# An encoder layer in float32: the low parts of half of the w_up blocks made in an earlier stage and kept in DRAM

## The chip, the cores and the metric

The kernel runs on one core of one Trainium2 chip. The metric is the time of one execution on the device, in microseconds (us), of a program that has all inputs in DRAM and writes both outputs to DRAM. A core has five engines with an instruction queue each: PE (matrix products), DVE (vector), ACT (scalar functions and casts), POOL (a second vector engine) and SP (which only issues transfers). Each engine takes its instructions in order; semaphores order the engines among each other. DMAs are issued by SP and ACT on hardware queues and by POOL on a software queue.

## The reference

One layer for 1536 tokens (512 of a prompt and 1024 of a sample), model width 1024, hidden width 4096, in float32. What the change touches is the last part:

```python
h = rms_norm(x, g_mix)
...
merged = jax.nn.sigmoid(ga) * (attn @ w_branch_a) + jax.nn.sigmoid(gb) * (sgu @ w_branch_b)
x = x + merged @ w_out
h2 = rms_norm(x, g_mlp)
x = x + jnp.square(jax.nn.relu(h2 @ w_up)) @ w_down
...
return rms_norm(x, g_final)
```

## The kernel before

**Products.** Every operand of a float32 product is split into a high part, hi (ACT casts it to float32r), and a rest, lo (DVE subtracts: lo = raw - hi). A product is then three matmuls: hi by hi, hi by lo and lo by hi. `weight` (L156) loads a weight tile of 128x512 (256 KB) with SP into a ring of three buffers (`raw`, N_RAW = 3), lets ACT cast it (L153) and DVE subtract (L154) into rings of five (`hi`, `lo`, N_SPLIT = 5). A raw buffer is free when ACT and DVE have both read it, hi and lo when PE has used them.

**Stages.** Projections, spatial gating and attention fill 0 to 1184 us; gates and the two branches, in three chunks of 512 tokens, 1184 to about 1614; w_out, the residual and the norm up to about 1770; the MLP the rest. In the gates stage a chunk has 14 gate products of 24 matmuls, 8 products of branch a of 12 and 8 of branch b of 24.

**MLP.** Both products use a scheme with seven products in place of eight for 2x2 blocks. The seven forms are p1, p2, q3 and q4 to q7; the sums of weight blocks for q4 to q7 (`up_sums`, `down_sums`) are made by DMA during attention. Group g (two, 768 tokens each) runs over c = 0 to 7; each c has two blocks of `up_products`, here called even (j = 0) and odd (j = 1), of seven weights each in the order p1, q6, q7, p2, q5, q4, q3 (UP_ORDER), 12 matmuls of 384 columns per weight, and then `down_products` with 14 weights. Names with a prime below: p1', q6' are weights of the odd block.

Between the products of an up block the results are combined and split: p1 is copied by ACT (L933); v = q6 - p1 (L936), z = v - q7 (L943); a11 is the squared Relu of p1 + p2 (ACT L915, L916), then cast (ACT) and subtracted (DVE) into act; a22 = z + q5 (DVE L946), a21 (L951), a12 (L956), and sums of them (L862 to L873) likewise. q3 accumulates on the PSUM bank of q5, so PE may start q3 only when DVE has read q5 for a22. In `down_products` POOL adds z to two tiles after q7 (L995, L996) and the kept p to one after q3 (L1006).

**Forms of the normed rows.** h2 (the normed rows, transposed) is stored to `h2_scr`; `diff_steps` reads it back and stores sums of blocks to `form_scr`. `form_steps` loads the seven forms of a group with POOL (`raw_form`, L1026, 28 loads) and splits them into `hf`. For group 0 that happens ahead of and within the first up block; for group 1 in the odd block and the down products of the last c of group 0. In group 1 POOL also loads finished rows of group 0 (`row`, L1061) and the gain (`g_final`, L240) and stores the normed rows.

**What sets the order.** Instructions stand in program order as written, moved by the scheduler of the tile framework; `side` steps are dealt out one after each product. The waits come from the buffers' rings.

Of the kernel before, what the change touches and what calls it, by code (L numbers as in the profile page):

```python
# [10 lines left out]
F32 = mybir.dt.float32  # L11
# [97 lines left out]
def encoder_kernel(ctx: ExitStack, tc: tile.TileContext, a):  # L109
# [25 lines left out]
    gate_scr = [dram.tile([P, NTOK], F32, name=f"gate_scr{m}") for m in range(EARLY)]  # L135
    form_scr = [dram.tile([len(DIFFS), 4, P, HT], F32, name=f"form_scr{g}") for g in range(2)]
    row_scr = dram.tile([GT, DM], F32, name="row_scr")
    h2_scr = dram.tile([KB, P, NTOK], F32, name="h2_scr")
    x1_scr = dram.tile([NTOK, DM], F32, name="x1_scr")
    up_sums = {k: dram.tile([DM // 2, DFF // 2], F32, name=f"up_{k}") for k in SUMS}  # L140
    down_sums = {k: dram.tile([DFF // 2, DM // 2], F32, name=f"down_{k}") for k in SUMS}
# [11 lines left out]
        nc.scalar.copy(hi, src)  # L153
        eng.tensor_sub(lo, src, hi.bitcast(F32))  # L154

    def weight(src, k, pair=None, eng=nc.vector):  # L156

        raw = wp.tile([P, 512], F32, tag="raw", name="raw", bufs=N_RAW).rearrange("p (k n) -> p k n", k=k)
        nc.sync.dma_start(out=raw, in_=src.rearrange("(k p) n -> p k n", p=P))
        if pair is None:  # L160
            pair = (wp.tile([P, 512], F32R, tag=s, name=s, bufs=N_SPLIT) for s in ("hi", "lo"))
        hi, lo = (t.rearrange("p (k n) -> p k n", k=k) for t in pair)
        split(hi, lo, raw, eng)
        return hi, lo

    def stationary(src, col, nk):
# [3 lines left out]
    def product(out, terms):  # L170

        for _ in product_steps(out, terms):
            pass
# [470 lines left out]
    def resident2(name):  # L644
        return res2.tile([P, 4, 512], F32R, tag="res2", name=name)

    with ExitStack() as ph:
        fp = ph.enter_context(tc.tile_pool(name="gates", bufs=20))
        rp = ph.enter_context(tc.tile_pool(name="rows", bufs=1))

        def half_tile(name):
            return fp.tile([P, 512], F32, tag="half", name=name)

        def merge_attention(t):

            r = rp.tile([P, NG, NPAIR, ROW], F32, tag="rows", name="rows")
            for g in range(NG):
                nc.sync.dma_start(out=r[:, g], in_=o_scr[g][t * P:(t + 1) * P])
            low = r[:, :, :, 128:130]
            den = r[:, :, :, 130:132]  # L660
            m = small.tile([P, NPAIR, 2], F32, tag="m", name="m")
            nc.vector.tensor_tensor(out=m, in0=low[:, 0], in1=low[:, 1], op=ALU.min)
            nc.vector.tensor_tensor(out=m, in0=m, in1=low[:, 2], op=ALU.min)
            e = small.tile([P, NG, NPAIR, 2], F32, tag="e", name="e")
            for g in range(NG):
                nc.vector.tensor_sub(e[:, g], m, low[:, g])
            nc.scalar.activation(e, e, AF.Exp)
            s = small.tile([P, NG, NPAIR, 2], F32, tag="s", name="s")
            for g in range(NG):
                nc.vector.tensor_mul(s[:, g], e[:, g], den[:, g])  # L670
            nc.vector.tensor_add(m, s[:, 0], s[:, 1])
            m2 = small.tile([P, NPAIR, 2], F32, tag="m2", name="m2")
            nc.vector.tensor_add(m2, m, s[:, 2])
            nc.vector.reciprocal(m2, m2)
            for g in range(NG):
                nc.vector.tensor_mul(e[:, g], e[:, g], m2)
            att, tmp = half_tile("att"), half_tile("att_g")
            for g in range(NG):
                dst = (tmp if g else att).rearrange("p (q h c) -> p q h c", q=NPAIR, h=2)
                nc.vector.tensor_mul(  # L680
                    dst, r[:, g, :, 0:128].rearrange("p q (h c) -> p q h c", h=2),
                    e[:, g, :, :, None].to_broadcast([P, NPAIR, 2, 64]))
                if g:
                    nc.vector.tensor_add(att, att, tmp)
            return att

        for n in range(NCH):
            sig = {}
            attT = tuple(resident2(f"att_{s}") for s in "hl")
            for i in range(2 * KB):  # L690
                s, m = divmod(i, KB)
                if i % 3 == 0 and i < 12:
                    att = merge_attention(4 * n + i // 3)
                sig[s, m] = half_tile("sig")
                if i < EARLY:
                    acc = sig[s, m]
                    nc.sync.dma_start(out=acc, in_=gate_scr[m][:, n * 512:(n + 1) * 512])
                else:
                    w = stationary(w_in, (C_GB, C_GA)[s] + m * P, KB)
                    acc = acc_tile()  # L700
                    product(acc, feature_terms(w, hT[n]))
                nc.scalar.activation(sig[s, m], acc, AF.Sigmoid)
                if i % 3 == 2 and i < 12:
                    to_features(att, [attT], 4 * n + i // 3)
            sgu = resident()
            for k in range(KB):
                raw = half_tile("sgu_raw")
                nc.sync.dma_start(out=raw, in_=sgu_scr[k][:, n * 512:(n + 1) * 512])
                hi, lo = sgu[k // 4]
                split(hi[:, k % 4, :], lo[:, k % 4, :], raw)  # L710
            for m in range(KB):
                w = stationary(a["w_branch_a"][0], m * P, 4)
                acc = acc_tile()
                product(acc, feature_terms(w, [attT]))
                nc.vector.tensor_mul(sig[1, m], acc, sig[1, m])
            for m in range(KB):
                w = stationary(a["w_branch_b"][0], m * P, KB)
                acc = acc_tile()
                product(acc, feature_terms(w, sgu))
                nc.vector.tensor_mul(sig[0, m], acc, sig[0, m])  # L720
                nc.vector.tensor_add(sig[0, m], sig[0, m], sig[1, m])
            hT[n] = resident()
            for m in range(KB):
                hi, lo = hT[n][m // 4]
                split(hi[:, m % 4, :], lo[:, m % 4, :], sig[0, m])
# [13 lines left out]
    def h_features(t, halves):  # L739

        for i, h in enumerate(halves):
            pt = tp_tile()
            for b in range(4):
                nc.tensor.transpose(pt[:, b * P:(b + 1) * P], h[:, b * P:(b + 1) * P], ident)
            hT2 = pp.tile([P, 512], F32, tag="half", name="h2T", bufs=2)
            nc.vector.tensor_mul(
                hT2.rearrange("p (k t) -> p k t", k=4), pt.rearrange("p (k t) -> p k t", k=4),
                g_mlp[:, 4 * i:4 * i + 4, None].to_broadcast([P, 4, P]))
            nc.sync.dma_start(
                out=h2_scr[4 * i:4 * i + 4, :, t * P:(t + 1) * P].rearrange("k p t -> p k t"),  # L750
                in_=hT2.rearrange("p (k t) -> p k t", k=4))

    def diff_steps(g, k, new, eng, wait):
# [2 lines left out]

        def load(key, r, s):
            x[key] = new()
            eng.dma_start(out=x[key], in_=h2_scr[4 * s + k, :, g * GT + r * HT:g * GT + (r + 1) * HT])

        def store(form, key):
            eng.dma_start(out=form_scr[g][DIFFS.index(form), k], in_=x[key])
# [26 lines left out]
    for k in range(4):  # L789

        room = [x1[(2 * k + i // 2) % 6][:, i % 2 * HT:(i % 2 + 1) * HT] for i in range(4)]
        sums += diff_steps(0, k, lambda room=room: room.pop(0), nc.gpsimd, 0)
    for ch in range(2):
        cols = slice(ch * 512, (ch + 1) * 512)
        w = {}
# [103 lines left out]
    def slab_view(s):  # L899
        return s.rearrange("p a b c -> p (a b c)").bitcast(F32)[:, :DM]  # L900

    def block_of(w, sums, form, rows, cols, r, c):

        if form in SUMS:
            return sums[form][r, c]
        i, j = {"p1": (0, 0), "p2": (1, 0), "q3": (1, 1)}[form]
        return w[i * rows + r.start:i * rows + r.stop, j * cols + c.start:j * cols + c.stop]

    def up_products(hf, j, forms, between):

        c = slice(j * P, (j + 1) * P)
        held = {}

        def squared(x, src):
# [1 line left out]
            nc.scalar.activation(x, x, AF.Square)  # L916

        for form in UP_ORDER:
            w = weight(block_of(a["w_up"][0], up_sums, form, DM // 2, DFF // 2, slice(0, DM // 2), c), 4)
            on = {"p2": "p1", "q3": "q5"}.get(form)  # L920
            acc = held[on] if on else bank()
            held[form] = acc
# [88 lines left out]
    def form_source(g, form, k):  # L1011
        if form in DIFFS:
            return form_scr[g][DIFFS.index(form), k]
        r, s = {"p1": (0, 0), "p2": (0, 1), "q4": (1, 1)}[form]
        return h2_scr[4 * s + k, :, g * GT + r * HT:g * GT + (r + 1) * HT]

    def form_steps(g, fs):

        items = [(form, k) for form in UP_ORDER for k in range(4)]
        raws = {}  # L1020

        def step(i):
            for j in range(i, min(i + N_FORM, len(items))):
                if j not in raws:
                    raws[j] = unit("raw_form")
                    nc.gpsimd.dma_start(out=raws[j], in_=form_source(g, *items[j]))  # L1026
            form, k = items[i]
            fs[k].put(form, raws[i])

        return [lambda i=i: step(i) for i in range(len(items))]  # L1030
# [131 lines left out]
```

## Time and profile before

| | us |
|---|---|
| median of three runs | 2805.28 (2803.55 to 2806.35) |
| profiled execution | 2803.75 |
| its span, first to last instruction | 2802.0 |
| PE busy | 2692.5 |
| DVE busy | 1747.7 |
| ACT busy | 1290.1 |
| POOL busy | 422.5 |

The mean granted PE clock over the span is 0.986 of full speed. A PE matmul of 384 columns in the MLP takes 0.17 us of its queue, an up block's weight (12 of them) 2.1 us. In the profile's rows, "x" counts instructions, the name ahead of "<-" is what is written, behind it what is read (buffer numbers left out), and square brackets give how long the engine stood idle before the row and what ended that.

### The profile page before, as it was taken

How to read it: one execution, taken by the hardware profiler on the slowest of the kernel's cores; microseconds unless marked ns; L12 is line 12 of the kernel's file. 1: busy time of each engine (PE TensorE's matmuls, PEld its weight loads, DVE VectorE, ACT ScalarE, POOL GpSimd, SP SyncE). 2: the span in 40 equal slices, each digit the busy share in tenths (PEclk: the TensorE clock that was granted, in tenths of full speed). 3: DMA queues.
4: the chain of work that ended last, by engine and by line, in shares of the span. 5: the costliest groups of instructions: out<-in, count | busy, mean ns of one | idle time of the engine just before them, and what ended most of it. 6: DMA issues, size and time to landing. Idle time of an engine off the chain costs nothing.

```text
span 2802.0 us, 38921 instructions
## 1 busy us (share of the span) xinstructions
PE 2692.5 (96%) x13400; PEld 2309.0 (82%) x13400; DVE 1747.7 (62%) x3722; ACT 1290.1 (46%) x2766; POOL 422.5 (15%) x507
## 2 busy tenths in 40 slices
PE   7999999999999999999999999899999989999997
PEld 5788888888888887888888887788989878888886
DVE  5542200166666666556555526788888868888888
ACT  5421111255556566553434321555556545555555
POOL 1000000011121212100000002222211322222222
PEclk9999999999999999999999999899999989999998
DMA  3112222247576768554443437654544555444443
GB/s 128 53 49 75 89 76 79 87 112 179 151 176 180 174 174 193 132 153 140 136 144 119 141 118 244 229 150 146 152 143 129 161 189 156 141 142 136 139 143 128
DMA packets 376439, 391.16 MB, mean 140 GB/s; under 512 B 23088, under 2 KB 290352, under 8 KB 372656
## 3 DMA queue, kind: packets, MB, share of 16 engines
q1 hardware_dynamic: 337008, 253.85, 30.3%
q0 software_dynamic: 28112, 86.83, 12.8%
q10 hardware_dynamic: 11120, 47.98, 5.0%
q8 instruction: 106, 1.74, 0.3%
q14 instruction: 93, 0.76, 0.1%
HBM read 333.22 MB, written 122.45 MB: 163 GB/s over the span
## 4 chain that ended last, share of the span: by engine, by line
PE 35%; DVE 8%; DMA 6%; issue 4%; ACT 4%; POOL 3%; DVEq 0%; SPq 0%; ACTq 0%; POOLq 0%
PE acc L979 7%; PE acc L178 7%; PE acc L180 7%; PE acc L179 7%; PE acc L928 6%; DVE lo L154 3%; DMA raw<-up_q 3%; ACT hi L153 1%; POOL x L996 1%; POOL x L995 1%; DVE act L154 1%; DMA raw<-in_w_down_dram 1%; ACT a L916 1%; ACT a L915 1%; ACT act L153 1%
## 5 line engine op out<-in xcount | busy, mean ns | idle before, releaser
L154 DVE TENSOR_TENSOR lo<-raw,hi 128x512 fp32r<-128x512 f32 x695 | 556.2, 805 | 420.8 <-ACT hi L153 413.8
L153 ACT CAST hi<-raw 128x512 fp32r<-128x512 f32 x696 | 430.6, 619 | 686.4 <-PE acc L179 238.3
L178 PE MATMUL acc<-res_h,hi 128*128 128x512 f32 x1344 | 556.2, 414 | 0.8 <-DVE stg L579 0.8
L180 PE MATMUL acc<-res_h,lo 128*128 128x512 f32 x1344 | 526.5, 392 | 0.0
L179 PE MATMUL acc<-res_l,hi 128*128 128x512 f32 x1344 | 525.3, 391 | 0.0
L928 PE MATMUL acc<-hf,hi 128*128 128x384 f32 x1792 | 471.6, 344 | 46.0 <-DVE a L946 24.8
L979 PE MATMUL acc<-hi,act 128*128 128x512 f32 x1344 | 423.9, 395 | 6.6 <-ACT hi L153 6.6
L928 PEld LDWEIGHTS acc<-hf,hi 128*128 128x128 f32 x1792 | 331.8, 193 | 59.2 <-ACT hi L153 30.8
L979 PEld LDWEIGHTS acc<-hi,act 128*128 128x128 f32 x1344 | 255.6, 191 | 61.4 <-ACT hi L153 8.9
L928 PE MATMUL acc<-hf,lo 128*128 128x384 f32 x896 | 306.1, 342 | 0.0
L180 PEld LDWEIGHTS acc<-res_h,lo 128*128 128x128 f32 x1344 | 252.4, 188 | 54.5
L179 PEld LDWEIGHTS acc<-res_l,hi 128*128 128x128 f32 x1344 | 254.3, 189 | 36.0
L178 PEld LDWEIGHTS acc<-res_h,hi 128*128 128x128 f32 x1344 | 254.0, 189 | 36.4 <-DVE stg L579 0.9
L979 PE MATMUL acc<-lo,act 128*128 128x512 f32 x672 | 266.1, 396 | 5.1 <-DVE lo L154 5.1
L551 ACT ACTIVATE pr<-pr,stg 128x128 f32<-128x128 f32 (+2 forms) x288 | 125.9, 438 | 175.8 <-DVE stg L548 139.5
L928 PEld LDWEIGHTS acc<-hf,lo 128*128 128x128 f32 x896 | 172.9, 193 | 0.9 <-DVE lo L154 0.8
L979 PEld LDWEIGHTS acc<-lo,act 128*128 128x128 f32 x672 | 128.3, 191 | 34.5 <-DVE lo L154 8.0
L521 DVE TENSOR_TENSOR q<-qT,q 64x256 fp32r<-64x256 f32 x288 | 120.7, 419 | 47.7 <-ACT q L518 43.9
L573 PEld LDWEIGHTS o<-v,pT 128*128 128x128 f32 x896 | 120.4, 191 | 24.9 <-DVE pT L563 14.7
L563 DVE COPY pT<-tp 128x512 f32<-128x512 f32 (+1 forms) x144 | 82.2, 571 | 93.9 <-PE tp L561 92.8
L995 POOL TENSOR_TENSOR x<-x,z 128x512 f32<-128x512 f32 x48 | 70.5, 1469 | 426.9 <-DVE z L994 426.8
L573 PE MATMUL o<-v,pT 128*128 128x64 f32 x896 | 117.3, 268 | 7.9 <-DVE pT L563 7.7
(186 smaller groups left out, 4119.9 us busy)
## 6 DMA issues: line engine op xcount, KB each, us to landing
raw<-in_w_in_dram SPq DMA_DIRECT2D x192, 256.0 KB, 3.0
raw<-up_q SPq DMA_DIRECT2D x128, 256.0 KB, 2.9
raw<-down_q SPq DMA_DIRECT2D x128, 256.0 KB, 2.7
raw<-in_w_up_dram SPq DMA_DIRECT2D x96, 256.0 KB, 2.9
raw<-in_w_down_dram SPq DMA_DIRECT2D x96, 256.0 KB, 2.9
up_q<-in_w_up_dram POOLq DMA_DIRECT2D x32, 512.0 KB, 9.3
down_q<-in_w_down_dram POOLq DMA_DIRECT2D x32, 512.0 KB, 10.9
raw<-in_w_branch_b_dram SPq DMA_DIRECT2D x48, 256.0 KB, 2.8
```

Source lines behind the costliest of these rows:

```text
L153: nc.scalar.copy(hi, src)
L154: eng.tensor_sub(lo, src, hi.bitcast(F32))
L178: nc.tensor.matmul(out, sh, mh, start=i == 0, stop=False)
L179: nc.tensor.matmul(out, sh, ml, start=False, stop=False)
L180: nc.tensor.matmul(out, sl, mh, start=False, stop=i == n - 1)
L521: nc.vector.tensor_sub(q2[rows, h, 1, :], src, q2[own, h, 0, :].bitcast(F32))
L551: last_of["act"] = nc.scalar.activation(pr[:, h, at:at + kn], pr[:, h, at:at + kn], AF.Exp, bias=low, scale=-1.0, accum_out=stg[:, j, 130 ...
L563: nc.vector.tensor_copy(self.pT[:, :n], pt[:, :n])
L573: nc.tensor.matmul(o[:, (2 * j + h) * 64:(2 * j + h + 1) * 64], self.pT[:, q * P:(q + 1) * P], found["v"][:, slot, h * 64:(h + 1) * 64], s ...
L928: nc.tensor.matmul(acc, st, mv, start=not on and k == 0 and n == 0, stop=k == 3 and n == 2, skip_group_check=bool(on))
L979: nc.tensor.matmul(acc, st, mv, start=not on and k == 0 and n == 0, stop=k == 1 and n == 2, skip_group_check=bool(on))
L995: nc.gpsimd.tensor_sub(x21, x21, z)
```

## The change

It has five parts.

1. In the gates stage `next_rest` runs after each of the gate products and the branch-b products: it takes the block of w_up loaded at the call before, casts it (ACT), subtracts (DVE), stores the rest to DRAM (`up_rest`) with POOL, and issues the load of the next block with POOL. 56 blocks, the seven forms of the eight odd j, are made that way, at 66 call places.
2. In the MLP the odd blocks' weights get lo by a POOL DMA from `up_rest` into the same ring, in place of DVE's subtraction: 7 per c, 112 in all. The raw load on SP and ACT's cast stay.
3. `h2_scr` becomes one tensor for each group.
4. The loads of each of the four lists of `diff_steps` for group 0 stand four places earlier in `sums`.
5. The 28 form loads of group 1 are issued by SP, those of group 0 still by POOL. `block_of` moves up unchanged and gets a helper, `up_block`.

```diff
-    h2_scr = dram.tile([KB, P, NTOK], F32, name="h2_scr")
+    h2_scr = [dram.tile([KB, P, GT], F32, name=f"h2_scr{g}") for g in range(2)]
+    up_rest = dram.tile([len(FORMS), DFF // 2 // P // 2, P, 512], F32R, name="up_rest")
...
-    def weight(src, k, pair=None, eng=nc.vector):
+    def weight(src, k, pair=None, eng=nc.vector, rest=None):
...
-        split(hi, lo, raw, eng)
+        if rest is None:
+            split(hi, lo, raw, eng)
+        else:
+            nc.scalar.copy(hi, raw)
+            nc.gpsimd.dma_start(out=lo, in_=rest.rearrange("p (k n) -> p k n", k=k))
...
+        rests = [(form, j) for j in range(1, DFF // 2 // P, 2) for form in FORMS]
+        loaded = []
+
+        def next_rest():
+
+            if loaded:
+                form, j, raw = loaded.pop()
+                t = fp.tile([P, 512], F32R, tag="rest", name="rest", bufs=2)
+                nc.scalar.copy(t, raw)
+                nc.vector.tensor_sub(t, raw, t.bitcast(F32))
+                nc.gpsimd.dma_start(out=up_rest[FORMS.index(form), j // 2], in_=t)
+            if rests:
+                form, j = rests.pop(0)
+                raw = fp.tile([P, 512], F32, tag="whole", name="whole", bufs=1)
+                nc.gpsimd.dma_start(
+                    out=raw.rearrange("p (k n) -> p k n", k=4), in_=up_block(form, j).rearrange("(k p) n -> p k n", p=P))
+                loaded.append((form, j, raw))
...
                     product(acc, feature_terms(w, hT[n]))
+                    next_rest()
...
                 product(acc, feature_terms(w, sgu))
+                next_rest()
...
-        sums += diff_steps(0, k, lambda room=room: room.pop(0), nc.gpsimd, 0)
+        steps = diff_steps(0, k, lambda room=room: room.pop(0), nc.gpsimd, 0)
+
+        sums.insert(max(0, len(sums) - 4), steps[0])
+        sums += steps[1:]
...
-            w = weight(block_of(a["w_up"][0], up_sums, form, DM // 2, DFF // 2, slice(0, DM // 2), c), 4)
+            w = weight(up_block(form, j), 4, rest=up_rest[FORMS.index(form), j // 2] if j % 2 else None)
...
-                    nc.gpsimd.dma_start(out=raws[j], in_=form_source(g, *items[j]))
+                    (nc.gpsimd, nc.sync)[g].dma_start(out=raws[j], in_=form_source(g, *items[j]))
```

**First place: DVE in the even block of c = 2 of group 1.** Before, from the last addition of the down products of c = 1 (L1004) on; the six lo are those of q5, q4, q3, p1', q6' and q7', in this order:

```order
L1004 TENSOR_TENSOR x_20697<-x_20697,acc_21550 128x512
L154 TENSOR_TENSOR lo_21725<-raw_21722,hi_21724 128x512
L154 TENSOR_TENSOR lo_21750<-raw_21747,hi_21749 128x512
L936 TENSOR_TENSOR v_21676<-acc_21663,p1_21647 128x384
L154 TENSOR_TENSOR lo_21785<-raw_21782,hi_21784 128x512
L943 TENSOR_TENSOR z_21697<-v_21676,acc_21684 128x384
L154 TENSOR_TENSOR lo_21814<-raw_21811,hi_21813 128x512
L154 TENSOR_TENSOR lo_21835<-raw_21832,hi_21834 128x512
L154 TENSOR_TENSOR act_21627<-a11_21717,act_21627 128x384
L946 TENSOR_TENSOR a22_21741<-z_21697,acc_21728 128x384
L154 TENSOR_TENSOR lo_21860<-raw_21857,hi_21859 128x512
```

The same place of the changed kernel (L1033 is the addition, L975 a22):

```order
L1033 TENSOR_TENSOR x_21035<-x_21035,acc_21888 128x512
L155 TENSOR_TENSOR lo_22063<-raw_22060,hi_22062 128x512
L155 TENSOR_TENSOR lo_22088<-raw_22085,hi_22087 128x512
L965 TENSOR_TENSOR v_22014<-acc_22001,p1_21985 128x384
L155 TENSOR_TENSOR lo_22123<-raw_22120,hi_22122 128x512
L972 TENSOR_TENSOR z_22035<-v_22014,acc_22022 128x384
L155 TENSOR_TENSOR act_21965<-a11_22055,act_21965 128x384
L975 TENSOR_TENSOR a22_22079<-z_22035,acc_22066 128x384
```

The subtractions for p1', q6' and q7' are gone; those of q5, q4 and q3 keep their places.

**Second place: ACT and POOL there.** ACT of the changed kernel, from the cast of q3 on (L167 are casts of the odd block's weights; L944, L945 are Relu and square of a11):

```order
L154 CAST hi_22122<-raw_22120 128x512
L167 CAST hi_22151<-raw_22149 128x512
L167 CAST hi_22172<-raw_22170 128x512
L944 ACTIVATE a11_22055<-acc_21972 128x384
L945 ACTIVATE a11_22055<-a11_22055 128x384
L154 CAST act_21965<-a11_22055 128x384
```

This order is that of before, line numbers apart: both casts of the odd block still stand ahead of a11. POOL of the changed kernel, in the next lines of its queue after the last additions of the down products (L1035) and the row loads:

```order
L1090 DMA row_21352<-row_scr_97 128x512
L1035 TENSOR_TENSOR x_21035<-x_21035,p_21102 128x512
L168 DMA lo_21513<-up_rest_100 128x512
L168 DMA lo_21534<-up_rest_100 128x512
L168 DMA lo_21559<-up_rest_100 128x512
L168 DMA lo_21580<-up_rest_100 128x512
L168 DMA lo_21615<-up_rest_100 128x512
L168 DMA lo_21642<-up_rest_100 128x512
L168 DMA lo_21679<-up_rest_100 128x512
L1107 DMA out_y_prompt_dram<-row_21348 128x512
```

These rows are those of c = 1; all c of group 1 with row loads are alike. Before, nothing stood between the last addition (L1006) and the stores of the rows (L1078).

**Third place: SP at the down products of the last c of group 0.** Before, its queue held weights alone:

```order
L159 DMA raw_20083<-down_q4_107 128x512
L159 DMA raw_20125<-down_q6_106 128x512
L159 DMA raw_20131<-down_q6_106 128x512
L159 DMA raw_20173<-down_q7_105 128x512
L159 DMA raw_20179<-down_q7_105 128x512
```

Now the form loads of group 1 stand among them:

```order
L160 DMA raw_20421<-down_q4_109 128x512
L1055 DMA raw_form_20233<-form_scr1_96 128x384
L1055 DMA raw_form_20260<-form_scr1_96 128x384
L1055 DMA raw_form_20289<-form_scr1_96 128x384
L160 DMA raw_20463<-down_q6_108 128x512
L160 DMA raw_20469<-down_q6_108 128x512
L1055 DMA raw_form_20328<-form_scr1_96 128x384
L1055 DMA raw_form_20360<-h2_scr1_99 128x384
```

Nine more form loads follow before the first weight of q7.

More of the change, by code (lines that the diff above doesn't have):

```diff
@@ L645, in resident2, with block_of, up_block @@
         return res2.tile([P, 4, 512], F32R, tag="res2", name=name)
+    def block_of(w, sums, form, rows, cols, r, c):
+        if form in SUMS:
+            return sums[form][r, c]
+        i, j = {"p1": (0, 0), "p2": (1, 0), "q3": (1, 1)}[form]
+        return w[i * rows + r.start:i * rows + r.stop, j * cols + c.start:j * cols + c.stop]
+    def up_block(form, j):
+        return block_of(a["w_up"][0], up_sums, form, DM // 2, DFF // 2, slice(0, DM // 2), slice(j * P, (j + 1) * P))
     with ExitStack() as ph:
         fp = ph.enter_context(tc.tile_pool(name="gates", bufs=20))
+        rests = [(form, j) for j in range(1, DFF // 2 // P, 2) for form in FORMS]
[13 more added lines that the diff above has]
+                loaded.append((form, j, raw))
         rp = ph.enter_context(tc.tile_pool(name="rows", bufs=1))
@@ L749, in h_features @@
             nc.sync.dma_start(
-                out=h2_scr[4 * i:4 * i + 4, :, t * P:(t + 1) * P].rearrange("k p t -> p k t"),
+                out=h2_scr[t // 6][4 * i:4 * i + 4, :, t % 6 * P:(t % 6 + 1) * P].rearrange("k p t -> p k t"),
                 in_=hT2.rearrange("p (k t) -> p k t", k=4))
@@ L758, in load @@
             x[key] = new()
-            eng.dma_start(out=x[key], in_=h2_scr[4 * s + k, :, g * GT + r * HT:g * GT + (r + 1) * HT])
+            eng.dma_start(out=x[key], in_=h2_scr[g][4 * s + k, :, r * HT:(r + 1) * HT])
         def store(form, key):
@@ L900, in slab_view @@
         return s.rearrange("p a b c -> p (a b c)").bitcast(F32)[:, :DM]
[L902 to L907, printed above, removed]
     def up_products(hf, j, forms, between):
-        c = slice(j * P, (j + 1) * P)
         held = {}
@@ L1014, in form_source @@
         r, s = {"p1": (0, 0), "p2": (0, 1), "q4": (1, 1)}[form]
-        return h2_scr[4 * s + k, :, g * GT + r * HT:g * GT + (r + 1) * HT]
+        return h2_scr[g][4 * s + k, :, r * HT:(r + 1) * HT]
     def form_steps(g, fs):
```

## The prediction

> **What bounds the kernel now.** First the page's busy times and the windows by stage.
>
> ```profile
> span 2802.0 us, 38921 instructions
> PE 2692.5 (96%) x13400; PEld 2309.0 (82%) x13400; DVE 1747.7 (62%) x3722; ACT 1290.1 (46%) x2766; POOL 422.5 (15%) x507
> ```
> ```profile
> core 0: us, PE busy (x) PEld busy (x) DVE busy (x) ACT busy (x) POOL busy (x), PEclk, DMA share, GB/s
> 1184.00:1350.00 166.00, 165.52 (x741) 136.63 (x740) 99.10 (x234) 77.53 (x122) 0.89 (x2) 1.00 0.49 148
> 1850.00:1910.00 60.00, 58.98 (x300) 53.44 (x299) 49.63 (x83) 33.18 (x63) 13.97 (x9) 1.00 0.50 149
> 2210.00:2290.00 80.00, 67.06 (x295) 56.32 (x295) 61.91 (x104) 41.72 (x88) 31.25 (x42) 0.91 0.61 193
> 2464.00:2526.00 62.00, 58.59 (x290) 53.26 (x289) 52.94 (x88) 33.59 (x66) 14.39 (x16) 0.97 0.48 141
> ```
>
> PE is the bound: in the gates (first window) it is never free; in the MLP it is free 1 us of 60 in group 0, 3.4 of 62 in group 1, and 12.9 of 80 between the groups. DVE is the next engine (85% in the last window), but 62% over the span: only those PE gaps can be won. The waits by PE, window by window (1184:1663, 1790:2199, 2199:2344, 2344:2770), say what ended them:
>
> ```profile
> PE tp L248 <- DVE att L684: 0.5, 1, 0.5
> ```
> ```profile
> PE acc L928 <- ACT p L933: 3.6, 5, 0.7
> PE acc L928 <- DVE a L946: 3.4, 4, 1.7
> ```
> ```profile
> PE acc L979 <- ACT hi L153: 5.1, 4, 2.9
> PE acc L979 <- DVE lo L154: 4.9, 4, 2.0
> ```
> ```profile
> PE acc L928 <- DVE a L946: 18.2, 6, 3.5
> PE acc L928 <- ACT p L933: 3.5, 6, 1.4
> ```
>
> Group 1 loses 18.2 us in six waits, one in each of c = 1 to 6, all for a22 (L946) ahead of the product q3 of the **even** block. After each, PE runs slowly for a while: in the third c three matmuls took 0.52 us before the wait (two in 0.51, overlapping the third) and about 1 us after it, which makes q3's four threes some 1.5 us longer.
>
> ```profile
> 2421.17 0.51 PE L928 MATMUL acc<-hf,hi 128*128 128x384 f32 x2
> ...
> 2425.11 0.98 PE L928 MATMUL acc<-hf,hi 128*128 128x384 f32 x2 [3.26 <-DVE a L946]
> ...
> 2426.21 0.84 PE L928 MATMUL acc<-hf,hi 128*128 128x384 f32 x2
> ```
>
> Why a22 is late there, in the timelines of POOL, DVE and ACT:
>
> ```profile
> 2412.10 1.28 POOL L1006 TENSOR_TENSOR x<-x,p 128x512 f32<-128x512 f32 x1 [6.46 <-DVE x L1004]
> 2413.68 0.55 POOL L1061 DMA_DIRECT2D row<-row_scr  x1 [0.30 <-POOL x L1006]
> ...
> 2416.43 1.30 POOL L1006 TENSOR_TENSOR x<-x,p 128x512 f32<-128x512 f32 x1
> ```
> ```profile
> 2410.71 0.69 DVE L154 TENSOR_TENSOR lo<-raw,hi 128x512 fp32r<-128x512 f32 x1 [1.77 <-ACT hi L153]
> ...
> 2414.45 3.83 DVE L154 TENSOR_TENSOR lo<-raw,hi 128x512 fp32r<-128x512 f32 x2
> ...
> 2423.94 0.56 DVE L154 TENSOR_TENSOR act<-a,act 128x384 fp32r<-128x384 f32 x1 [0.79 <-ACT act L153]
> ```
> ```profile
> 2420.58 0.62 ACT L153 CAST hi<-raw 128x512 fp32r<-128x512 f32 x1 [2.05 <-DMA raw<-in_w_up_dram]
> 2421.81 0.62 ACT L153 CAST hi<-raw 128x512 fp32r<-128x512 f32 x1 [0.61 <-DMA raw<-up_q]
> 2422.33 0.48 ACT L915 ACTIVATE a<-acc 128x384 f32<-128x384 f32 x1
> ```
>
> The subtractions of q5 and q4 (2414.45, two) take 3.83 us beside POOL's additions, against 0.69 alone. Only when the second ends, at 2418.28, is a raw buffer (ring of 3) free for the odd block's q6, which lands at 2421.8, 3.5 us later. ACT casts it at 2421.81, and that cast stands ahead of a11's Relu (2422.33); DVE's act of a11 and then a22 follow, and PE goes on at 2425.11. The chain is: POOL's additions, lo of the **even** block, ring, load, ACT's order.
>
> **The change part by part.** The sum stands against the profiled execution, 2803.75 us (span plus 1.75), itself 1.5 below the median of 2805.28.
>
> *112 subtractions leave DVE.* By the rows below, 872 ns each in the MLP, 98 us of DVE work; alone, as in the gates, 689 ns.
>
> ```profile
> L154 DVE TENSOR_TENSOR lo<-raw,hi 128x512 fp32r<-128x512 f32 x439 | 380.4, 872 | 76.4 <-ACT hi L153 75.2
> ```
> ```profile
> L154 DVE TENSOR_TENSOR lo<-raw,hi 128x512 fp32r<-128x512 f32 x155 | 106.0, 689 | 108.3 <-ACT hi L153 106.0 <-PE tp L248 2.0
> ```
>
> On PE's path this is worth almost nothing in the steady state. The orders above the prediction show why: two lo of the odd block go from before a22, but at 2423.94 DVE was waiting for ACT (0.79), not working them off. What ACT has ahead of a11, both casts of odd-block weights, stays, and their raw loads still wait for lo of q5 and q4. I take 0; the ends are -18.2 - 6 x 1.5 = -27 for group 1 (all waits gone) and 0. PE's waits for L933 (3.6 and 3.5) hang on the same ACT chain: 0.
>
> *112 loads of lo on POOL's queue*, 256 KB each: 29 MB more. Issuing costs 0.55 us (row 2413.68), 62 us of an idle engine. Seven stand behind the last L1006, which ends at 2417.73; the first two buffers are free by then (PE is past q7 and p2), so both loads start near 2418 and, by the row<-row_scr below, land about 3.8 us later, near 2422, where PE would want the first after q3, near 2424 without any wait: a margin of 2. But they fly beside the raw load that ends the chain (2418.28 to 2421.8). The DMA views of 1850:1970, 2412:2428 and 2340:2770 price that:
>
> ```profile
> raw<-in_w_up_dram SPq DMA_DIRECT2D x12, 256.0 KB, 2.8
> ```
> ```profile
> raw<-in_w_up_dram SPq DMA_DIRECT2D x4, 256.0 KB, 3.6
> raw<-up_q SPq DMA_DIRECT2D x4, 256.0 KB, 3.2
> row<-row_scr POOLq DMA_DIRECT2D x2, 256.0 KB, 3.7
> ```
> ```profile
> row<-row_scr POOLq DMA_DIRECT2D x12, 256.0 KB, 3.8
> ```
>
> Beside POOL's row loads a raw load takes 3.2 to 3.6 instead of 2.8: +0.4 to +0.8, and I take 0.7. It adds to a22's wait in the six c that wait in group 1 (+4.2) and in the four of group 0 (+2.8): **+7**; ends 0 (lo flies after the raw load) and twice 0.8 in 13 c, +21.
>
> The Trainium skill, "DMA: Bandwidth & Descriptors", section "SWDGE vs HWDGE vs iDMA", speaks against the change: the software and hardware queues have queues of their own inside each DMA engine, which takes turns between them. The slower raw loads beside POOL's (3.6 against 2.8) agree; by full turns with two loads of lo the time would be rival B's, below.
>
> *The gates* get 56 rests: a load, a cast (0.62), a subtraction (0.69), a store. PE is full there; 24 matmuls of a product take 24 x 165.52 / 741 = 5.4 us, while one rest's round with its single buffer is 3.8 + 0.62 + 0.69 + 0.55 = 5.7. ACT would fall behind 0.3 us a product, 17 us over 56; but it is free for 88 of 166 us, holds five weights (2.5 products) ahead, and the 24 products of branch a, half as long, carry no rest. I take 0; ends 0 and +17.
>
> *Between the groups* the 28 form loads pass from POOL to SP, among the raw loads.
>
> ```profile
> 2249.46 0.54 POOL L1026 DMA_DIRECT2D raw_form<-form_scr  x1 [1.86 <-DVE hf L154]
> 2254.60 1.29 POOL L995 TENSOR_TENSOR x<-x,z 128x512 f32<-128x512 f32 x1 [4.61 <-DVE z L994]
> ```
> ```profile
> 2242.94 0.62 ACT L153 CAST hi<-raw 128x512 fp32r<-128x512 f32 x1 [3.59 <-DMA raw<-down_q]
> ```
>
> POOL wins nothing: its last form load is 4.6 us before it has other work. SP now queues each weight behind form loads that wait for DVE and ACT; but DVE loses the odd block's lo there, and the raw load for which ACT waited 3.59 us can start earlier. PE's waits are 10.0 us here (5.1 + 4.9): I take **-3**, ends -10 and +8 (the same waits again, from SP's queue). The first c of group 0 has three queues to settle (POOL's form loads behind a lo that waits for PE, DVE lighter): 0, ends -4 and +4.
>
> *Loads of sums ahead*: one store's issue, 0.55 us, off a PE wait: **-0.5**. The split tensor of normed rows removes no wait that PE ends on: 0.
>
> Sum: +7 - 3 - 0.5 = +3.5, so 2807.
>
> **The rivals.**
> *A, DVE was the limit after all* (85% busy in group 1): with 112 fewer subtractions the next block's lo start earlier, miss POOL's additions, and the ring runs ahead. Point: q4's lo must end by 2415 instead of 2418.28. Price: 27 in group 1, 10 between the groups: 2766; half of it 2785. Against: DVE waits for ACT at 2410.71, so it is not behind there. For: the ends of several c are this close. 2775, chance 0.27.
> *B, the software queue slows the critical raw load by two loads, not by one*: 13 c x 1.6 = +21, with -3.5: 2821. It decides if lo's first two loads are issued before the raw load lands, which 2417.73 allows. Against: POOL may stand waiting for a buffer and issue the second late. Chance 0.20.
> *C, the rests hold the gates up*: 17 us on PE, with the rest 2824. Chance 0.08.
>
> **How the numbers follow.** The forecast, 0.45, lies between 2798 and 2815. A measurement of this kernel tells 0.2%, 5.6 us, from no change; so 2799.7 to 2810.9 is "same". Faster: 0.09 of the forecast and 0.25 of A, 0.34. Slower: 0.08 of the forecast, 0.17 of B and 0.06 of C, 0.31. Same: the rest, 0.35. Range: 2775 to 2823 leaves out A's better part and the worse ends of B and C, about a tenth on each side.
>
> **What would show it.** PE's six waits for a22 in group 1 stay, at 3.5 to 4 us each (forecast), over 4.5 (B), or under 1.5 (A). raw<-up_q there takes 3.5 or more; ACT's cast ahead of a11 still ends on that load. PE in the gates stays without gaps (against C). If DVE falls by about 60 us (98 less the rests' 39) and the time stays, the relief was off the path. The forecast is wrong if the raw loads of the odd block start earlier than lo of q4 now lets them.

## The result and the profile after

The changed kernel takes 2896.9 us (median of four, 2895.3 to 2899.7), the kernel before 2805.8 beside it: a ratio of 1.0327, interval 1.0309 to 1.0345. It is 3.3% slower, and outside the predicted range (2775 to 2823).

The page of the changed kernel begins:

```profile
span 2897.9 us, 39437 instructions
PE 2726.2 (94%) x13400; PEld 2319.2 (80%) x13400; DVE 1706.3 (59%) x3666; ACT 1314.8 (45%) x2822; POOL 540.5 (19%) x703
```

The span grew by 95.9 us. DVE lost 41 us of work, where the prediction worked out some 60 (98 less 39): the MLP's subtractions of weights went from 383.2 to 305.1 us, 78 us for 112 of them, so those that left took 0.7 us each and not the mean of 872 ns. No gain from it is to be seen. The first product of the MLP dates the loss; PE's timelines of before and of after:

```profile
1774.75 0.69 PE L928 MATMUL acc<-hf,hi 128*128 128x384 f32 x1 [5.89 <-ACT hf L153]
```
```profile
1854.88 0.69 PE L957 MATMUL acc<-hf,hi 128*128 128x384 f32 x1 [5.73 <-ACT hf L154]
```

So 80.1 us are lost ahead of the MLP, and 95.9 - 80.1 = 15.8 in it.

**Ahead of the MLP.** The windows of the gates, columns as in the prediction:

```profile
1184.00:1350.00 166.00, 147.07 (x611) 115.24 (x610) 86.25 (x206) 68.08 (x114) 30.55 (x47) 0.96 0.65 191
1350.00:1520.00 170.00, 149.52 (x599) 116.79 (x600) 91.60 (x193) 71.12 (x122) 32.43 (x50) 0.93 0.64 186
1520.00:1663.00 143.00, 134.34 (x576) 108.18 (x575) 74.44 (x141) 58.47 (x100) 10.93 (x17) 0.96 0.52 151
```

PE did 611 matmuls in the first 166 us where it had done 741, and it was idle for 19 us only: its matmuls were slower too, at a granted clock of 0.93 to 0.96 where it had been 1.00. From 1184 us to the MLP PE was idle for 62.4 us (16.1 before) and busy for 608.5 (574.7 before) with the same products: 46.3 and 33.8 make up the 80.1. Its main waits (1184:1700), where there had been one of 0.5 us, are for hi and lo of its own weights:

```profile
PE acc L183 <- ACT hi L154: 20.3, 17, 2.7
PE acc L185 <- DVE lo L155: 17.5, 9, 4.1
```

ACT and DVE are no busier than before in the first two windows. The row of the rests' casts (duration, first and last start) and ACT's waits in the gates (1184:1663) tell what they did instead:

```profile
L672 ACT CAST rest<-whole x56: 614/620/622, 1197.7 to 1580.3; 128x512 fp32r<-128x512 f32 x56
```
```profile
ACT rest L672 <- DMA whole<-up_q: 72.4, 23, 6.4
ACT rest L672 <- DMA whole<-in_w_up_dram: 59.2, 17, 6.6
ACT rest L672 <- issue: 52.8, 10, 6.8
```

Some 184 us of ACT's time went by in front of 50 of the 56 casts, 131.6 of them put down to the load; for the 52.8 under "issue" the profile names no releaser. One rest follows another after (1580.3 - 1197.7) / 55 = 6.96 us. The timelines of ACT and POOL show one round, and what stands behind it on ACT:

```profile
1292.93 0.62 ACT L672 CAST rest<-whole 128x512 fp32r<-128x512 f32 x1 [5.64 <-DMA whole<-in_w_up_dram]
1293.46 0.61 ACT L154 CAST hi<-raw 128x512 fp32r<-128x512 f32 x1
1293.98 2.18 ACT L154 CAST res_h<-sgu_raw 128x512 fp32r<-128x512 f32 x4
1296.06 0.61 ACT L154 CAST hi<-raw 128x512 fp32r<-128x512 f32 x1
1299.84 0.62 ACT L672 CAST rest<-whole 128x512 fp32r<-128x512 f32 x1 [3.17 <-DMA whole<-in_w_up_dram]
```
```profile
1294.57 0.55 POOL L674 DMA_DIRECT2D up_rest<-rest  x1 [6.50 <-DVE rest L673]
1295.11 0.75 POOL L678 DMA_DIRECT2D whole<-in_w_up_dram  x1
1301.48 0.55 POOL L674 DMA_DIRECT2D up_rest<-rest  x1 [5.62 <-DVE rest L673]
```

Cast at 1292.93, subtraction, store issued at 1294.57, next load issued at 1295.11, landed at 1299.84, next cast. Meanwhile the casts of PE's own weights stand behind the rest. DVE's queue is held in the same way: 146.9 us of its idle time lie in front of 51 of the rests' subtractions, which wait for ACT's cast.

**In the MLP.** PE's waits in c = 1 to 6 of group 1 (2428:2870), against 18.2 before:

```profile
PE acc L957 <- DVE a L975: 29.2, 6, 6.8
PE acc L957 <- ACT p L962: 3.5, 6, 1.7
```

The third c again, now at 2494 (ACT's timeline, then the DMAs issued in 2494:2514):

```profile
2506.52 0.62 ACT L167 CAST hi<-raw 128x512 fp32r<-128x512 f32 x1 [2.22 <-DMA raw<-in_w_up_dram]
2510.41 0.62 ACT L167 CAST hi<-raw 128x512 fp32r<-128x512 f32 x1 [3.26 <-DMA raw<-up_q]
2510.93 0.48 ACT L944 ACTIVATE a<-acc 128x384 f32<-128x384 f32 x1
```
```profile
raw<-up_q SPq DMA_DIRECT2D x6, 256.0 KB, 3.1
lo<-up_rest POOLq DMA_DIRECT2D x4, 256.0 KB, 5.7
raw<-in_w_up_dram SPq DMA_DIRECT2D x3, 256.0 KB, 4.6
```

The chain is the one of the prediction, with a longer load in it. SP issued q6's raw load at 2504.05, and it landed for the cast at 2510.41: 6.4 us where it had taken 3.5. The two POOL loads of lo ahead of it began at 2503.38. In four of the six c both lo loads are issued ahead of it like this, and it takes 6.0 to 6.9 us; at c = 3 one is ahead, and it takes 3.9. The six waits grew by 11.0 us (18.2 to 29.2). By counts of PE's matmuls c = 1 to 6 of group 1 took some 392 us against 381, its c = 0 some 72 against 66, and group 0 was no longer than before (501 against 504).

### The profile page after: what moved, and what is told of

Its sections match the earlier page's. It is cut to its first block, busy times and chain, and to the rows that moved or that the text cites. A ratio compares the mean times of both kernels' runs of the same rounds, so it can differ in the third digit from the quotient of the medians.

```text
span 2897.9 us, 39437 instructions
## 1 busy us (share of the span) xinstructions
PE 2726.2 (94%) x13400; PEld 2319.2 (80%) x13400; DVE 1706.3 (59%) x3666; ACT 1314.8 (45%) x2822; POOL 540.5 (19%) x703
## 5 line engine op out<-in xcount | busy, mean ns | idle before, releaser
L155 DVE TENSOR_TENSOR lo<-raw,hi 128x512 fp32r<-128x512 f32 x583 | 476.9, 823 | 332.8 <-ACT hi L154 328.7
L154 ACT CAST hi<-raw 128x512 fp32r<-128x512 f32 x584 | 358.8, 619 | 491.9 <-PE acc L184 104.1
L183 PE MATMUL acc<-res_h,hi 128*128 128x512 f32 x1344 | 563.5, 419 | 13.4 <-ACT hi L154 12.5
L185 PE MATMUL acc<-res_h,lo 128*128 128x512 f32 x1344 | 534.1, 397 | 11.6 <-DVE lo L155 10.9
L183 PEld LDWEIGHTS acc<-res_h,hi 128*128 128x128 f32 x1344 | 258.1, 192 | 55.0 <-ACT hi L154 18.1
L672 ACT CAST rest<-whole 128x512 fp32r<-128x512 f32 x56 | 34.7, 620 | 200.0 <-DMA whole<-up_q 72.4
```

The lines of the kernel that those rows point to most:

```text
L183: nc.tensor.matmul(out, sh, mh, start=i == 0, stop=False)
L185: nc.tensor.matmul(out, sl, mh, start=False, stop=i == n - 1)
```

## The experiments

Each kernel is the changed one with the edit shown, unless it says "before". Ratios are to the kernel before in the same series, with 95% intervals.

**1. Two loads under way.**

```diff
-            if loaded:
-                form, j, raw = loaded.pop()
+            if len(loaded) == 2 or loaded and not rests:
+                form, j, raw = loaded.pop(0)
...
-                raw = fp.tile([P, 512], F32, tag="whole", name="whole", bufs=1)
+                raw = fp.tile([P, 512], F32, tag="whole", name="whole", bufs=2)
```

> The changed kernel, but with two loads of w_up blocks under way in the gates stage (two buffers 'whole', each rest is made from the load issued two calls before). Same traffic, same casts, subtractions and stores. Theory 1 (the round of one rest through one buffer, about 6.8 us against 5.4 us of a product, holds ACT and so PE): the MLP starts within 5 us of before (first product of the MLP near 1775 us instead of 1855), total 2812 to 2822. Rival (the added traffic slows the weights' own loads, or the added casts and subtractions are too many): the MLP still starts at 1840 to 1855, total 2880 to 2897.

Measured: 2870.3 us, 1.0228 (1.0213 to 1.0244). The MLP started at 1825.9. Neither theory was right: 29 of the 80 us came back.

```profile
L672 ACT CAST rest<-whole x56: 610/621/642, 1197.8 to 1420.9; 128x512 fp32r<-128x512 f32 x56
```

The rests now follow each other after 4.1 us, but all of them had gone by 1421. The scheduler had put one rest to about each weight cast on ACT, so that they took turns with half products (12 matmuls, 2.7 us) and not with whole ones. What was missing from the theory is the order; runs 5 and 6 test it.

**2. Gates alone**: the rests are made and stored, and the MLP subtracts on DVE.

```diff
-        if rest is None:
+        if True:
             split(hi, lo, raw, eng)
```

> The changed kernel makes and stores the rests, but the MLP subtracts on DVE as before and does not load them. Theory: the loss has two parts, gates (80 us) and MLP (16 us); this keeps the first alone: MLP starts at 1855, total 2878 to 2886, and the a22 waits of group 1 are again 3 us each. Rival (the MLP's loss comes from the form loads on SP or from the split tensor): total 2890 to 2897.

Measured: 2880.6 us, 1.0266 (1.0245 to 1.0286); MLP from 1851.7 on, 1025.4 us long (before 1027.3). The two parts are apart: 77 us in the gates, and the MLP as before.

**3. The three small parts alone**: as 2, and `next_rest` returns at once.

> Only the split tensor of normed rows, the loads of sums ahead and the form loads of group 1 on SP; no rests are made or loaded. Theory: these three are worth little, total 2796 to 2807 (the prediction had -3.5). Rival (form loads on SP hold up the weights behind them): the change of group slower by 5 us or more, total 2808 to 2815.

Measured: 2803.3 us, 0.9984 (0.9974 to 0.9994). The small gain that was predicted for them.

**4. Five of seven**: as 1, and p1 and q6 of the odd block subtracted on DVE.

```diff
-            w = weight(up_block(form, j), 4, rest=up_rest[FORMS.index(form), j // 2] if j % 2 else None)
+            w = weight(up_block(form, j), 4, rest=up_rest[FORMS.index(form), j // 2] if j % 2 and form not in ("p1", "q6") else None)
```

> As the run with two loads under way in the gates, and in the MLP the rests of p1 and q6 of the odd block are subtracted on DVE as before; only the other five of each odd block are loaded. Theory B (the loads of these two fly beside the raw load of q6 that ends the a22 chain): the a22 waits of group 1 fall back from 5.7 to 6.8 us to 3 to 3.5 us, total 8 to 16 us below the run with two loads under way. Rival (the waits grew because of POOL's queue or the general traffic of the 112 loads): they stay over 5 us, total within 4 us of it.

Measured: 2849.3 us, 1.0154 (1.0139 to 1.0169), 21 below run 1; the MLP took 1025.1 us against 1042.8 (the other 4.3 lie ahead of it, where the edit changes nothing). The a22 waits were back (18.1 us in five). The MLP is as long as that of run 2, which loads no rests (1025.4). So without the first two loads the cost in the MLP is gone, and the five others, 80 subtractions fewer, gain nothing.

**5. Spread**: as 1, with each rest's cast tied in ACT's order behind the last weight cast of its own product.

```diff
-            split(hi, lo, raw, eng)
+            tied["hi"] = nc.scalar.copy(hi, raw)
+            eng.tensor_sub(lo, raw, hi.bitcast(F32))
...
-                nc.scalar.copy(t, raw)
+                with tc.issue_after(tied["hi"].ins):
+                    nc.scalar.copy(t, raw)
```

> The run with two loads under way, and each rest's cast tied behind the last weight cast of the product that it is written after, so that ACT's order has one rest to two weight casts and none in branch a (in the run with two loads the scheduler had moved them to one rest to about one weight cast). Theory 1 in its new form (what ACT waits in a rest's turn, times how densely the rests stand in ACT's order, sets the loss): with 3.5 to 4 us a rest against 5.4 us of a product the gates lose under 10 us, MLP starts at 1775 to 1785, total 2815 to 2828. Rival (traffic or added work in the gates): MLP starts at 1810 or later, total over 2850.

Measured: 2824.4 us, 1.0061 (1.0044 to 1.0077); MLP from 1780.5 on. Its gates' windows, with the same 56 rests and all their traffic:

```profile
1184.00:1350.00 166.00, 161.18 (x714) 133.25 (x715) 107.77 (x240) 84.66 (x139) 33.85 (x52) 0.99 0.73 215
1350.00:1520.00 170.00, 170.00 (x763) 140.85 (x762) 110.44 (x246) 89.13 (x149) 34.97 (x54) 1.00 0.75 223
```

PE is full again in the second at a DMA share of 0.75, higher than in the changed kernel (0.64). Traffic was not the cause.

**6. Tied, but with one buffer**: the edit of 5 without that of 1.

> The changed kernel with its one buffer, and only each rest's cast tied behind the last weight cast of its product (as in the spread run), so that branch a has no rests. It tells the buffer from the order. Theory (a rest's turn through one buffer is 6.8 us against 5.4 us of a product, whatever the order; the products of a chunk that carry rests are slowed, branch a's are not and cannot give it back): MLP starts at 1825 to 1860, total 2868 to 2900. Rival (the scheduler's crowding was all): MLP starts under 1790, total under 2832.

Measured: 2882.8 us, 1.0263 (1.0243 to 1.0284); MLP from 1830.8 on. Order alone gives 24 us, the second buffer alone 29, both together 74 of the 80.

**7. Spread, five of seven**: 5 with the edit of 4.

> As the spread run, and the odd block's p1 and q6 are subtracted on DVE, the other five loaded. Theory: gates as in the spread run, MLP as in the earlier run with five loads (1025 us from its first product to the end): total 2798 to 2810, that is no gain over before although 80 subtractions have left DVE in the MLP. Rival (DVE's relief is worth something once the gates are free): under 2795.

Measured: 2808.9 us, 1.0003 (0.9993 to 1.0014). With the rests out of the gates' way and the two harmful loads gone, 80 subtractions less and 80 loads more are together worth nothing: the MLP took 1026.3 us against 1027.3 before.

**8. Only the first two loaded**: 7, with `form in ("p1", "q6")` in place of `form not in`.

> The spread run with only the rests of p1 and q6 of the odd block loaded (on POOL), the other five subtracted on DVE. The counterpart of the run with the other five. Theory (these two loads beside q6's raw load are the whole cost in the MLP): a22 waits of 4 to 6 us in group 1 and total 2815 to 2826, near the spread run's 2824. Rival (it takes all seven): total 2808 to 2814.

Measured: 2835.4 us, 1.0084 (1.0066 to 1.0102): more than expected, above run 5. The DMA view of its c = 1 of group 1 (2355:2375) and PE's a22 waits in c = 1 to 6:

```profile
raw<-up_q SPq DMA_DIRECT2D x5, 256.0 KB, 4.9
...
lo<-up_rest POOLq DMA_DIRECT2D x2, 256.0 KB, 6.0
```
```profile
PE acc L960 <- DVE a L978: 34.7, 6, 6.9
```

Two loads do all of it. Why five subtractions on DVE beside them cost 11 us more (its four times lie between 2826.5 and 2841.5, and the profile is of the longest) was not followed up.

**9. Before, with a raw buffer of its own for q6 of the odd block** (and 11 form buffers in place of 12).

```diff
...
+                       own=(lambda: mp.tile([P, 512], F32, tag="own", name="own", bufs=1)) if j % 2 and form == "q6" else None)
```

> The kernel before with one change: the raw load of the odd block's q6 has a buffer of its own (one form buffer fewer, 11 in place of 12), so that it no longer waits for q4's subtraction. Theory (the chain of the prediction: q4's lo, ring, q6's load, ACT's cast, a11, a22): the six a22 waits of group 1 fall from 3 us to 1 to 2 us (p1's load, which waits for q5's lo, ends the chain then), total 5 to 20 us below before. Rival (something else holds a22): waits as before, total within 4 us.

Measured: 2794.9 us, 0.9947 (0.9930 to 0.9964). The a22 waits fell from 18.2 to 14.8, less than expected; p1's load, the next in the chain, still waits for q5's subtraction. The total fell by far more than these 3.4 us: in the profile the MLP is 10.9 us shorter, 7.3 of them less busy time of PE for the same work (953.9 us against 961.2). Why its matmuls took less time was not followed up.

**10. Before, with POOL's additions of p on DVE** (`nc.vector.tensor_add` after q3).

> The kernel before with the three additions of the kept p after each down product's q3 on DVE in place of POOL. Theory (POOL's additions stretch the lo of q5 and q4 and so the a22 chain): those lo take 0.7 us each, but DVE has 2 us more to do ahead of them; the a22 waits fall by 1 to 2 us each, total 2790 to 2803. Rival (the stretch is not what delays q6's load): waits of 3 us or more, total 2805 to 2815.

Measured: 2802.0 us, 0.9975 (0.9964 to 0.9985); a22 waits 9.0 us in four, not 18.2 in six, but two new waits for ACT's cast of a weight (5.8). The stretch by POOL is real: with the additions on DVE two lo in a row take 1.29 us there (at 2423.79), where they had taken 3.83. How much of the chain it is stays open: the profiled execution was the longest of eight (2808.1), and its MLP is no shorter than before (1028.6 us against 1027.3).

**11. Two own buffers**: as 3, with own raw buffers for p1 and q6 of the odd block (ten form buffers).

> No rests; the three small parts of the change as in the run without rests, and raw buffers of their own for both p1 and q6 of the odd block (ten form buffers in place of twelve). Theory (ring of three raws ends the a22 chain): a22 waits of group 1 fall under 1 us, the small parts keep their 5 us, total 2778 to 2790, the fastest of all. Rival (with the ring out of the way the casts or the row loads hold a22): total 2790 to 2797.

Measured: **2775.8 us, 0.9882 (0.9868 to 0.9897)**, faster than both kernels. PE's waits in c = 1 to 6 of group 1:

```profile
PE acc L954 <- ACT p L959: 7.2, 10, 1.6
PE acc L954 <- DVE a L972: 2.3, 5, 0.5
```

The six waits of 3 us are gone, and the kernel is 28 us faster than run 3. This version still has part of the change: what is left out of it is the rests.

**12. As 11, with POOL's additions on DVE.**

> The run with two raw buffers of their own, and the additions of the kept p on DVE in place of POOL. With the a22 waits at 0.5 us the stretched lo of q5 and q4 should no longer matter: total within 5 us of 2776. Rival (the stretch still ends other waits, those for p1's copy or the first raw loads): 2762 to 2770.

Measured: 2788.0 us, 0.9924 (0.9908 to 0.9941), 12 slower than 11; both expectations missed it. In the profiles 6.4 of it lie in the MLP (1005.3 us against 998.9), where the a22 waits rose from 2.3 to 7.3 us, and the other 6 ahead of it, where the edit changes nothing. So where the chain has been cut, the move gains nothing and seems to harm.

**13. a11 first**: as 3, with the casts of p1 and q6 of the odd block tied behind a11's cast on ACT. No buffer is added.

```diff
...
+        if late:
+            with tc.issue_after(tied["a11"].ins):
+                split(hi, lo, raw, eng)
...
+                tied["a11"] = tied["cast"]
```

> The run without rests, with the casts of the odd block's p1 and q6 tied behind a11's cast in ACT's order; rings and loads as before. Theory (these casts ahead of a11 are what makes a22 late): the a22 waits of group 1 fall under 1 us, total 2772 to 2790. Rival (the loads themselves are too late for PE, so the wait moves to p1 and q6 of the odd block): total within 5 us of the run without rests, 2803.

Measured: 2779.3 us, 0.9897 (0.9882 to 0.9911); a22 waits 2.4 us in four. The order of two casts (24 us below run 3) was worth nearly as much as two buffers (28).

**14. Spread, a11 first**: the same tie in run 5, all seven rests on POOL's queue.

> The spread run (all rests loaded on POOL's queue) with the same order on ACT. Theory (POOL's loads cost something only because a cast that waits for the raw load of q6 stands ahead of a11): a22 waits under 1 us, total 2780 to 2795, within 10 us of the run with a11 first and no rests plus the 5 us that the spread rests cost in the gates. Rival (the slow raw loads then hold PE directly at p1 or q6): total over 2800.

Measured: 2833.7 us, 1.0088 (1.0071 to 1.0105). The rival was right. PE's waits in c = 1 to 6 of group 1:

```profile
PE acc L964 <- ACT p L969: 34.3, 10, 5.6
```

a22 is in time, but then the odd block's own casts come late, and PE waits for the copy of its p1 instead. It was not only the order on ACT that made the slow loads cost something.

**15. lo by SP**: run 5 with the seven rests of an odd block loaded on the hardware queue (`nc.sync.dma_start`, both sides seen as float32).

> The spread run with all seven rests of an odd block loaded by SP on the hardware queue, among the raw loads, in place of POOL's software queue. Same bytes at about the same time. If the bytes in flight make q6's raw load 6 us long: a22 waits of group 1 stay over 4.5 us, total 2815 or more. If it is POOL's software queue, or the descriptors that POOL writes: waits of 3 to 4 us, total 2800 to 2812.

Measured: 2808.3 us, 0.9999 (0.9989 to 1.0008), a22 waits 18.6. But SP had the first two lo behind q6's raw load.

**16. lo by SP, ahead**: each rest tied ahead of its raw load on SP.

> The spread run with the odd block's lo loaded by SP on the hardware queue, each issued ahead of its weight's raw load (in the earlier SP run the scheduler had put the first two behind q6's raw load). Theory order (any two loads of 256 KB issued ahead make q6's raw load 6 us long): a22 waits of group 1 over 5 us, total 2818 or more. Theory queue (it is POOL's software queue that slows the raw load): q6's raw load takes 4 us or less, waits of 3 to 4.5 us, total 2804 to 2814.

Measured: 2785.1 us, 0.9917 (0.9902 to 0.9932). Faster than either theory said, since the scheduler had also put a11 ahead of the two casts, as in 13; 14 was made as its counterpart on POOL's queue. The loads issued in c = 1 to 6 of group 1 in 16, then in 14:

```profile
raw<-up_q SPq DMA_DIRECT2D x53, 256.0 KB, 3.7
lo<-up_rest SPq DMA_DIRECT2D x49, 256.0 KB, 3.8
```
```profile
raw<-up_q SPq DMA_DIRECT2D x53, 256.0 KB, 4.4
lo<-up_rest POOLq DMA_DIRECT2D x49, 256.0 KB, 4.5
```

The same bytes with a11 first cost 49 us less on SP's queue than on POOL's, all of it in the MLP (1002.0 us against 1051.5). And 16's MLP is as long as that of run 13 without any rests (1001.7): loads that do not harm gain nothing either. Still mixed in it: on SP the first rest is issued some 2.5 us earlier. So it is not shown that the queue alone makes the difference.

## Why the prediction was wrong

**The step that failed is "I take 0; ends 0 and +17" for the rests in the gates.** It cost 80. Three things in it were wrong:

- *The round.* I added 3.8 + 0.62 + 0.69 + 0.55 = 5.7. Measured: 6.96. The loads of whole blocks landed 4.3 to 4.5 us after the start of their issue, not 3.8 as the row loads did (0.75 of it is the issue on POOL, where a row load's takes 0.55); the other 0.7 or so is what passes between the steps until the cast gets its turn on ACT, for which I had no term. Against 5.36 of a product that is 1.6 and not 0.3 each: 56 x 1.6 = 90, near the 80 measured.
- *The cover.* I counted ACT's idle time, its five weights ahead and branch a. But ACT takes its queue in order: a cast that waits for its load uses up idle time and holds every weight cast behind it. By this sum two and a half products of lead, 13 us, are gone after eight rests at 1.6.
- *The order.* "The 24 products of branch a carry no rest" was read from the source. In ACT's queue the scheduler had moved rests forward; branch a had its share, one to two weight casts. That could have been read before the run in the order of ACT, which I looked at for the MLP only. Of the 80 us the second buffer alone gives back 29 (run 1), the order alone 24 (run 6), and both together 74 (run 5): with either fault left, some 50 us remain.

As rival C, at 17 us and a chance of 0.08, the mechanism was named but mis-sized nearly fivefold.

**The loads of lo on POOL's queue, "+7; ends 0 and +21".** The mechanism was right and the size too small: 15.8 in the MLP, and 17.7 between runs 1 and 4. I took one load's delay of 0.7 us; both loads fly ahead of q6's raw load in four of the six c, and it takes 6.0 to 6.9 us instead of 3.5. The six waits of group 1 grew by 1.8 each on the mean; group 0, for which I had put 2.8, lost nothing. That is rival B in group 1, with its condition as I gave it (POOL's last addition ends early enough) and a chance of 0.20.

**"On PE's path this is worth almost nothing ... I take 0" for the subtractions** was right: run 7 is at 1.0003. Its 98 us were too many, since the mean of 872 ns holds the lo stretched beside POOL's additions, which stayed; 78 went. The chain of a22 was right too: the ring (9, 11) and ACT's order (13) shorten it, and so, less clearly, does POOL's stretch (10). I had put 27 us for all waits of group 1 gone; in runs 11 and 13 its c = 1 to 6 are some 21 and 19 us shorter than in run 3. Rival A's cause fell: no run with fewer subtractions on DVE gained from that.

**The small parts, -3 and -0.5**: run 3 measured about -4.5 (0.9984 of 2808). No run parts them from each other.

## What to carry to other kernels

Work that is added "beside" a full engine has to be looked up in the queue of each engine it passes: a short instruction whose operand is late holds all that stand behind it, and idle time of that engine is no cover. Compare the round of a load, its use and the reload of its single buffer with the cadence of the work beside it; if the round is longer, the difference is paid each time. And where a profile shows an engine waiting, follow the chain before relieving the engine that is busiest: two casts in another order (24 us, 0.9%) did what 112 subtractions less could not.

## What the runs showed of the hardware

- Two 256 KB loads on POOL's software queue, issued just ahead of a 256 KB load on SP's hardware queue, made it take 6.0 to 6.9 us where it took 3.5 in the same place without them, and 3.9 with one ahead. The Trainium skill, "DMA: Bandwidth & Descriptors", section "SWDGE vs HWDGE vs iDMA", has DMA engines take turns between the queues; turns would let a load on one queue wait for those on another, and these times agree. They do not single out turns as the cause: in run 16 two loads of the same size went ahead on SP's own queue, though one of them earlier, and the load behind them was cast within 3.3 to 5.2 us in c = 1 to 6.
- In the gates PE's matmuls slowed with gaps of up to 5.7 us between them: the granted clock was 0.93 to 0.96 in windows in which PE was busy 88 to 94% of the time. So the loss was larger than the gaps: up to the MLP 46.3 us more of idle time, and 33.8 us more of busy time for the same products.
- Two subtractions of 128x512 in a row on DVE took 3.83 us beside POOL's additions of the same shape and 1.29 us without them (run 10).
